# The rotary part of the latent queries: one matrix product, read crosswise, in place of two

## The chip, the cores and the metric

The kernel runs on 1 core of one Trainium2 chip. The metric is the device time of one execution in microseconds; times of several runs are given as their median.

## What is computed

Two layers of a trunk on 512 tokens of 1024 features. Each layer norms and modulates its input, makes one wide projection, runs three kinds of attention over it side by side (forgetting, latent and stick-breaking, 8 heads each), merges them through sigmoid gates, and ends with a SwiGLU network. The part that matters here is the query of the latent attention:

```python
cq = rms_norm(mla_ql, g_mla_q[l])                      # 512 x 384
q = to_heads(cq @ w_mla_uq[l], MLA_HEADS)              # 8 heads of 96
q_nope = q[..., :MLA_NOPE]                             # 64 plain
q_rope = apply_rope(q[..., MLA_NOPE:], cos[:, None], sin[:, None])   # 32 rotary

def apply_rope(x, cos, sin):
    x1, x2 = jnp.split(x.astype(jnp.float32), 2, axis=-1)
    out = jnp.concatenate([x1 * cos - x2 * sin, x1 * sin + x2 * cos], axis=-1)
```

So each rotary feature needs its own value times cos and the value of its partner, 16 features away, times sin with a sign.

## The kernel before

Features lie on the partitions and the 512 tokens on the free axis. Every float32 product is made of three passes on split numbers: `mm3` (lines 199 to 201) adds hi*hi, hi*lo and lo*hi, and `gemm` does that for each chunk of 128 input features. Weights are loaded by SP's queue four tiles deep; `divide` makes their hi with a copy on ScalarE (line 171) and their lo with a subtraction on VectorE (line 173), and runs two to three weights ahead of their use.

TensorE issues in the order in which the program is written. ScalarE, VectorE, GpSimd and the queues issue in an order that a scheduler finds at build time; the work of attention is given a lead of 30 in priority (`HP`).

The attention of a layer runs in windows, two heads each. The function `slot` goes through the eleven pieces of work of a head (the scores S of its four blocks of queries, and the transposes T and value products PV of the head before), and between them it takes steps from a queue of other matrix products: a step is three matmuls of one chunk, one unit of the queue has several. `left_steps` says how many steps the queue of a window has, and the slots spread them evenly.

Window 4 computes heads 6 and 7 (the last of the forgetting attention) and has the units `uqr` (rotary queries of latent heads 0 to 3), `uq` (plain queries of the first pair) and `ukv` (keys and values of the first pair). Window 5 computes heads 8 and 9, the first latent ones. Window 6 computes heads 10 and 11 and has the second `uqr` among its units. So there are two units of this kind in a layer, four in the kernel.

In `uqr`, the weights hold the rotary columns of four heads twice, 768 columns: once as they are, and once with the two halves of each head's 32 columns exchanged. Two products come out of it, of 128 features each. `rope_queries` multiplies the first by cos and the second by the signed sin (both with the scale of the scores) on VectorE, adds them on GpSimd, copies the hi part on ScalarE and subtracts for the lo part on GpSimd. `latent_head`, after the window, sends each head's 32 rows of hi and of lo to rows 64 to 95 of the tiles from which the head's scores are made; these transfers are issued by GpSimd. The score products of a latent head (lines 717 to 719) wait for them, and for the plain rows that lines 246, 247, 243 and 244 write.

Of the kernel before, what the change touches and what calls it, by code (L numbers as in the profile page):

```python
# [13 lines left out]
ALU = mybir.AluOpType  # L14
# [6 lines left out]
L = 2  # L21
# [11 lines left out]
# columns of the constants  # L33
C_INV, C_SGN, C_N = 0, 1, 2
# columns of the small vectors of a layer
# [4 lines left out]
# the blocks of queries whose weights ScalarE normalises  # L40
SCALE_ACT = {"f": (3,), "m": (2, 3)}
# between steps of the products: scores of a head (c), and transposes and products of the head before (p)
# [8 lines left out]
# products of constants that keep TensorE's clock up at the start  # L51
WARM = (24, 12)
# steps of products before each norm of the latents
WAIT = (8, 3, 8, 4)
# the chunk after which the rope tables are made
ROPE_AT = 4
# the chunk of the first products of the FFN after which the second half's norm comes
SS_AT = 3
# how far the work of attention goes before other work in the schedule, and steps by which the weights' division waits
HP, LAG = 30, 1  # L60

# 2*pi in parts of 8 bits, so that a product with a whole number below 2**16 is exact
# [4 lines left out]
def tile_hybrid_trunk(ctx: ExitStack, tc: tile.TileContext, xT, cvec, pos, cst, cmask, vec, gfin,  # L67
# [19 lines left out]
    # TensorE issues in the order written here; the other engines as the scheduler finds best  # L87
    ctx.enter_context(tc.manual_schedule(engines={pe.engine}))

    # ScalarE's functions, in phases of one table set each  # L90
# [15 lines left out]
    def windows(l):  # L106
        """Units of matrix products to run beside the attention of a pair of heads."""
        fox = [[("proj", l, 3 * p + i) for i in range(3)] for p in range(4)]
        sb = [[("proj", l, 12 + 3 * p + i) for i in range(3)] for p in range(4)]
        mla = [[("uqr", l, p // 2)] * (p % 2 == 0) + [("uq", l, p), ("ukv", l, p)] for p in range(4)]  # L110
        mg = [("merge", l, b, m) for b in range(3) for m in range(KC)]
        w = fox + [mla[0], mla[1] + [sb[0][0]], mla[2] + [sb[0][1]], mla[3] + [sb[1][0]], [sb[0][2], sb[1][1]]]
        w.append([mg[0], sb[1][2], mg[1], mg[2]])
        for p in range(2, 4):
            w.append([u for i in range(3) for u in (mg[3 * p - 3 + i], sb[p][i])])
        return w + [mg[9:14], mg[14:16], mg[16:]]

    def loads_of(u):
        kind, l, a = u[:3]
        if kind == "first":  # L120
            return [(w_first[l, a], NFIRST)]
        if kind == "proj":
            return [(w_proj[l, a], D)]
        if kind == "uqr":
            return [(w_uqr[l, a], 768)]
        if kind == "uq":
            return [(w_uq[l, a], 384)]
        if kind == "ukv":
            return [(w_ukv[l, a], 512)]
        if kind == "merge":  # L130
            return [(w_proj[l, 24 + a * KC + u[3]], D), (w_o[l, a * KC + u[3]], 512)]
        if kind == "out":
            return [(w_out[l, a], D)]
        if kind == "gu":
            return [(w_gu[l, a], D)]
        return [(w_dn[l, a, :, k0 * P : k1 * P], (k1 - k0) * P) for k0, k1 in KS]
# [22 lines left out]
    def divide(want, after=None):  # L159
        """hi and lo of the weights before the want-th; after: what goes before them on ScalarE and VectorE"""  # L160
# [17 lines left out]
    def W(unit, n=1, raw=3, ready=2, lag=0):  # L178
        """The next n weights, of that unit on, as (hi, lo); later ones are on their way."""
        i = at[0]  # L180
        if fourth[0]:
            raw, ready = 4, 3
        assert LOADS[i][0] == unit, (LOADS[i][0], unit)
        at[0] = i + n
        divide(i + n)

        def ahead():
            divide(i + max(n, ready + 1))
            fetch(i + max(n, raw + 1))

        if lag:
            later(lag, ahead)
        else:
            ahead()
        return splits[i] if n == 1 else splits[i : i + n]

# [6 lines left out]
    def gemm(o, wt, acts, m=P, start=True, stop=True, c0=0, cols=FULL):  # L203
        """o += W^T a over the chunks of acts, in steps; wt = (hi, lo) holds them m columns each from c0 on."""
# [19 lines left out]
    def steps(n):  # L224
        """n steps of the products in the queue"""
# [24 lines left out]
    H = S // 2  # L250

    class Norm:
        """1/sqrt(mean of squares over the features) of half the tokens, in every partition."""
# [77 lines left out]
    make_identity(nc, identf)  # L331
    # additive masks of the diagonal block: a query sees keys <= it, and keys < it
# [9 lines left out]
    # rope tables, rows alike in each 32: cos, and -sin | +sin  # L342
# [9 lines left out]
    # sin: +-r; cos: sin(pi/2 - |r|)  # L352
# [10 lines left out]
    def ada(l, i, c, wt=None, on_pool=False, after=None):  # L363
        """Column c of part i of the modulation."""
# [12 lines left out]
        if i in (1, 4):  # L377
            # g * (1 + scale)
# [16 lines left out]
    # ================= layers =================  # L395
    def values(ap, psv, name, got):
        """[2 heads' features, tokens] in PSUM -> [keys, block, head, hi | lo of the features]."""
# [14 lines left out]
    class Head:  # L412
# [4 lines left out]
        def S(self, i):  # L417
# [8 lines left out]
            if self.kind == "s":  # L426
                # sigmoid(z) of the key times the product of sigmoid(-z) over the later keys
# [20 lines left out]
        def T(self, js):  # L448
            """The weights of key blocks js, keys on the partitions, as hi and lo."""
# [12 lines left out]
        def PV(self, j):  # L462
            """[64 features, queries] += values^T weights^T; rows 0-63: hi of the values, rows 64-127: lo."""
# [12 lines left out]
    def slot(cur, prev, n):  # L476
        """The scores of a head and the rest of the head before it, between n steps of the queue."""
# [13 lines left out]
    for l in range(L):  # L491
# [32 lines left out]
        if l == 0:  # L524
# [4 lines left out]
            def warm(n):  # L529
                """Products of constants while there is nothing else: TensorE's clock falls when it idles."""  # L530
# [5 lines left out]
            # room that has no other use yet  # L536
# [65 lines left out]
        # of a head: qa = its queries' hi and lo, ka = its keys' hi twice; kb = its keys' lo  # L602
# [19 lines left out]
        def unit(u):  # L622
# [5 lines left out]
            elif kind == "uqr":  # L628
                wt = W(u, lag=LAG)
                ts = [pst("mm", f"tr{i}") for i in range(2)]  # L630
                yield from gemm(ts[0], wt, cq)
                yield
                yield from gemm(ts[1], wt, cq, c0=384)
                rope_queries(a, ts)
# [48 lines left out]
        def latent_keys(pr):  # L683
            """The rows that are alike in all heads"""
# [11 lines left out]
        def rope_queries(quad, ts):  # L696
# [4 lines left out]
            dve.scalar_tensor_tensor(qr, ts[0], sc, cosT, ALU.mult, ALU.mult)  # L701
            dve.scalar_tensor_tensor(qsf, ts[1], sc, sinT, ALU.mult, ALU.mult)
# [5 lines left out]
        def latent_head(pr):  # L708
            for hh in range(2):
                st_ = sets[pr % 2][hh * 4 : hh * 4 + 4]  # L710
                g = (pr % 2 * 2 + hh) * 32
                for a in range(2):
                    pool.dma_start(out=st_[a][64:96], in_=quads[pr // 2][a][g : g + 32])
# [28 lines left out]
        def merge(u, b, m):  # L742
            """merged[m] += sigmoid(gate) * (y_b w_o)"""
# [28 lines left out]
        def left_steps(w):  # L772
            n = {"proj": 8, "uqr": 6, "uq": 3, "ukv": 4, "merge": 12}
            return sum(n[u[0]] for u in win[w])

        # the first pair's projections, with the forget gates and the norms of the latents
        enqueue(0)
        steps(1)
        with scoped(f"fg{l}", "right") as lp:
            # log of the forget gates: min(z, 0) - ln(1 + exp(-|z|)); its sums, negated  # L780
# [183 lines left out]
def _inputs(x, c, positions, g_mix, w_ada, b_ada, w_in, b_fox_f, g_mla_q, w_mla_uq, g_mla_kv,  # L964
            w_mla_ukv, w_o_fox, w_o_mla, w_o_sb, w_out, g_ffn, w_ffn_gate, w_ffn_up, w_ffn_down, g_final):
    """The arrays of the launch: the inputs, laid out for it."""
# [5 lines left out]
    def tiles(w):  # L972
        # [L, K, N] -> [L, N / 128, 128 rows of a chunk, chunks, 128]
# [6 lines left out]
    def col(v):  # L980
        # [L, n * 128] -> [128, L, n]
# [6 lines left out]
    def qkv(w):  # L988
        # q, k, v tiles of a pair of heads, pair after pair
# [8 lines left out]
    uqr = np.stack([uq[..., 64:], np.concatenate([uq[..., 80:], uq[..., 64:80]], axis=-1)], axis=-2)  # L998
    # l kc p quad head part 32 -> l quad p part kc head 32
    uqr = uqr.reshape(L, 3, P, 2, 4, 2, 32).transpose(0, 3, 2, 5, 1, 4, 6).reshape(L, 2, P, 768)  # L1000
    ukv = np.asarray(w_mla_ukv).reshape(L, 2, P, 4, 2, 2, 64)  # l kc p pair head k|v 64
    ukv = ukv.transpose(0, 3, 2, 5, 1, 4, 6).reshape(L, 4, P, 512)

    wo = np.stack([np.asarray(w_o_fox), np.asarray(w_o_mla), np.asarray(w_o_sb)], axis=1)  # L 3 512 1024
# [15 lines left out]
    # row i: queries of the first half of block i; keys of its second half  # L1020
# [25 lines left out]
# 10000 ** (-i / 16) in float32  # L1046
# [25 lines left out]
```

## Time and profile before

| | |
|---|---|
| runs shown | 1897.41, 1897.56, 1901.94 us |
| median | 1897.56 us |
| span of the profiled execution, first to last instruction | 1895.3 us (that execution's own device time is not listed; the span is 2.3 us under the median) |
| TensorE busy | 1857.2 us, 98% |
| VectorE busy | 1169.2 us, 62% |
| ScalarE busy | 852.1 us, 45% |
| GpSimd busy | 141.8 us, 7% |

Busy time is the time covered by an engine's instructions. Matmuls are pipelined: one's record is longer than the distance to the next one's start. In the rows, L199 is line 199 of the kernel; a row of the timeline gives the start in us from the span's start, the duration in us, the engine, the line, the operation, the tile written and the tiles read, and shapes; idle time before it and what ended that stand in brackets.

### The profile page before, as it was taken

To read this page: it belongs to the slowest core of one execution; us is meant where nothing else is said; L and a number is where in the kernel's file an instruction comes from. 1 tells how busy PE (TensorE), PEld (TensorE's weight loads), DVE (VectorE), ACT (ScalarE), POOL (GpSimd) and SP (SyncE) were. 2 spreads that over 40 slices of the span, in tenths; PEclk is the share of its full clock that TensorE was granted. 3 is DMA by queue.
4 is the path that set the end of the run, shared out by engine and by line. 5 is a ranking of instruction groups with operands and counts; after the bars stand their busy time and mean duration, and the time that the engine had idled before them with its cause. 6 is when DMAs were issued, how large, how long until landed. Compare 5 with 4: busy or idle time off the path is not lost.

```text
span 1895.3 us, 24083 instructions
## 1 busy us (share of the span) xinstructions
PE 1857.2 (98%) x8956; PEld 1515.1 (80%) x8956; DVE 1169.2 (62%) x2043; ACT 852.1 (45%) x1543; POOL 141.8 (7%) x260
## 2 busy tenths in 40 slices
PE   6999999999999999999999999999999999999998
PEld 4788787777889888778897887777788888888887
DVE  8888887677756655554558898666664463333333
ACT  4767874443334322232237688544433342232321
POOL 4122100001000000000002121000110000000000
PEclk8999999999999999999999999999999999999999
DMA  7423323333642655555633222122142222223231
GB/s 276 141 73 81 82 79 117 102 110 131 208 150 70 211 177 184 171 184 194 197 107 101 66 68 85 66 84 83 68 145 99 97 100 100 95 95 98 92 92 53
DMA packets 76741, 224.22 MB, mean 118 GB/s; under 512 B 10768, under 2 KB 13968, under 8 KB 76624
## 3 DMA queue, kind: packets, MB, share of 16 engines
q1 hardware_dynamic: 69136, 213.30, 33.8%
q0 software_dynamic: 7488, 9.38, 2.5%
q8 instruction: 71, 1.16, 0.3%
q14 instruction: 46, 0.38, 0.1%
HBM read 209.20 MB, written 4.19 MB: 113 GB/s over the span
## 4 chain that ended last, share of the span: by engine, by line
PE 79%; DMA 9%; DVE 7%; issue 3%; ACT 2%; SPq 0%; DVEq 0%; POOL 0%; POOLq 0%
DMA wraw<-in_w_ada_dram 8%; PE gate L199 5%; PE gate L201 5%; PE gate L200 5%; PE proj L199 4%; PE proj L200 4%; PE dn L200 4%; PE dn L199 4%; PE dn L201 4%; PE proj L201 4%; PE o L199 3%; PE o L200 2%; PE o L201 2%; PE fu L200 2%; PE fu L199 2%
## 5 line engine op out<-in xcount | busy, mean ns | idle before, releaser
L171 ACT CAST wh<-wraw 128x1024 fp32r<-128x1024 f32 (+4 forms) x332 | 311.4, 939 | 560.3 <-PE fu L200 125.1
L173 DVE TENSOR_TENSOR wl<-wraw,wh 128x1024 fp32r<-128x1024 f32 (+4 forms) x332 | 375.8, 1132 | 230.0 <-ACT wh L171 224.7
L372 DVE CUSTOM_DVE_ANT_0 wraw<-wraw,condb 128x1024 f32<-128x1024 f32 x80 | 98.6, 1232 | 153.0 <-DMA wraw<-in_w_ada_dram 152.9
L199 PE MATMUL proj<-uh,wh 128*128 128x512 f32 x384 | 162.2, 422 | 0.0
L199 PE MATMUL gate<-uh,wh 128*128 128x512 f32 x384 | 157.8, 411 | 0.0
L201 PE MATMUL proj<-uh,wl 128*128 128x512 f32 x384 | 151.3, 394 | 0.0
L200 PE MATMUL proj<-ul,wh 128*128 128x512 f32 x384 | 151.3, 394 | 0.0
L201 PE MATMUL gate<-uh,wl 128*128 128x512 f32 x384 | 150.6, 392 | 0.0
L200 PE MATMUL gate<-ul,wh 128*128 128x512 f32 x384 | 150.6, 392 | 0.0
L199 PE MATMUL dn<-hh,wh 128*128 128x512 f32 (+1 forms) x396 | 145.5, 367 | 0.0
L200 PE MATMUL dn<-hl,wh 128*128 128x512 f32 (+1 forms) x396 | 145.4, 367 | 0.0
L201 PE MATMUL dn<-hh,wl 128*128 128x512 f32 (+1 forms) x396 | 144.4, 365 | 0.1
L201 PE MATMUL fu<-uh,wl 128*128 128x512 f32 x336 | 131.5, 391 | 1.6 <-DVE wl L173 1.6
L200 PE MATMUL fu<-ul,wh 128*128 128x512 f32 x336 | 131.0, 390 | 0.0
L199 PE MATMUL fu<-uh,wh 128*128 128x512 f32 x336 | 130.9, 389 | 0.0
L199 PE MATMUL fg<-uh,wh 128*128 128x512 f32 x320 | 125.5, 392 | 0.0
L200 PE MATMUL fg<-ul,wh 128*128 128x512 f32 x320 | 125.5, 392 | 0.0
L201 PE MATMUL fg<-uh,wl 128*128 128x512 f32 x320 | 125.5, 392 | 0.0
L199 PEld LDWEIGHTS gate<-uh,wh 128*128 128x128 f32 x384 | 72.0, 188 | 19.8 <-issue 4.8
L201 PEld LDWEIGHTS proj<-uh,wl 128*128 128x128 f32 x384 | 72.3, 188 | 16.9
L201 PEld LDWEIGHTS gate<-uh,wl 128*128 128x128 f32 x384 | 72.0, 188 | 16.7
L201 PEld LDWEIGHTS dn<-hh,wl 128*128 128x128 f32 x396 | 74.4, 188 | 13.3 <-DVE wl L173 0.5
(370 smaller groups left out, 3973.2 us busy)
## 6 DMA issues: line engine op xcount, KB each, us to landing
wraw<-in_w_proj_dram SPq DMA_DIRECT2D x96, 512.0 KB, 3.5
wraw<-in_w_gu_dram SPq DMA_DIRECT2D x88, 512.0 KB, 3.6
wraw<-in_w_ada_dram SPq DMA_DIRECT2D x80, 512.0 KB, 3.3
wraw<-in_w_dn_dram SPq DMA_DIRECT2D x32, 512.0 KB, 4.0
wraw<-in_w_o_dram SPq DMA_DIRECT2D x48, 256.0 KB, 2.6
wada<-in_w_ada_dram SPq DMA_DIRECT2D x16, 512.0 KB, 5.6
wraw<-in_w_out_dram SPq DMA_DIRECT2D x16, 512.0 KB, 3.5
wraw<-in_w_dn_dram SPq DMA_DIRECT2D x16, 384.0 KB, 3.1
```

Of the source, the lines that this page charges most:

```text
L171: ins = [act.copy(wh[:, :c], raws[j][:, :c]).ins]
L173: ins.append(dve.tensor_sub(wl[:, :c], raws[j][:, :c], wh[:, :c].bitcast(F32)).ins)
L199: pe.matmul(o, wh, ah, start=start, stop=False)
L200: pe.matmul(o, wh, al, start=False, stop=False)
L201: pe.matmul(o, wl, ah, start=False, stop=stop)
L372: ins = dve.tensor_tensor_reduce(out=wt, in0=wt, in1=condb, op0=ALU.mult, op1=ALU.add, scale=1.0, scalar=0.0, accum_out=m).ins
```

## The change

The weights of `uqr` hold each rotary column once, 384 columns, ordered so that the first halves of four heads fill features 0 to 63 and the second halves 64 to 127. One product comes out. VectorE multiplies it by cos as before; for the part with sin, two operations read the product crosswise: what goes to rows 0 to 63 is read from rows 64 to 127 and the other way round, with a constant per row (sign and scale) in a third column of the constants. Since a head's 32 rows now lie in two groups of 16, `latent_head` sends two transfers of 16 rows for each of hi and lo. The count of steps of the unit falls from 6 to 3 in `left_steps`, so the slots of windows 4 and 6 spread 10 and 18 steps in place of 13 and 21. The order of the columns of w_mla_uq and the new constants are prepared in `_inputs`.

```diff
-C_INV, C_SGN, C_N = 0, 1, 2
+C_INV, C_SGN, C_ROT, C_N = 0, 1, 2, 3
...
         if kind == "uqr":
-            return [(w_uqr[l, a], 768)]
+            return [(w_uqr[l, a], 384)]
...
             elif kind == "uqr":
-                wt = W(u, lag=LAG)
-                ts = [pst("mm", f"tr{i}") for i in range(2)]
-                yield from gemm(ts[0], wt, cq)
-                yield
-                yield from gemm(ts[1], wt, cq, c0=384)
-                rope_queries(a, ts)
+                t = pst("mm", "tr")
+                yield from gemm(t, W(u, lag=LAG), cq)
+                rope_queries(a, t)
...
-        def rope_queries(quad, ts):
+        def rope_queries(quad, t):
...
-            dve.scalar_tensor_tensor(qr, ts[0], sc, cosT, ALU.mult, ALU.mult)
-            dve.scalar_tensor_tensor(qsf, ts[1], sc, sinT, ALU.mult, ALU.mult)
+            dve.scalar_tensor_tensor(qr, t, sc, cosT, ALU.mult, ALU.mult)
+            for to, of in ((slice(0, 64), slice(64, 128)), (slice(64, 128), slice(0, 64))):
+                dve.scalar_tensor_tensor(qsf[to], t[of], csts[of, C_ROT : C_ROT + 1], sinT[of], ALU.mult, ALU.mult)
...
-                g = (pr % 2 * 2 + hh) * 32
+                g = (pr % 2 * 2 + hh) * 16
                 for a in range(2):
-                    pool.dma_start(out=st_[a][64:96], in_=quads[pr // 2][a][g : g + 32])
+                    for to, of in ((64, g), (80, 64 + g)):
+                        pool.dma_start(out=st_[a][to : to + 16], in_=quads[pr // 2][a][of : of + 16])
...
-            n = {"proj": 8, "uqr": 6, "uq": 3, "ukv": 4, "merge": 12}
+            n = {"proj": 8, "uqr": 3, "uq": 3, "ukv": 4, "merge": 12}
...
-    uqr = np.stack([uq[..., 64:], np.concatenate([uq[..., 80:], uq[..., 64:80]], axis=-1)], axis=-2)
...
-    uqr = uqr.reshape(L, 3, P, 2, 4, 2, 32).transpose(0, 3, 2, 5, 1, 4, 6).reshape(L, 2, P, 768)
+    uqr = uq[..., 64:].reshape(L, 3, P, 2, 4, 2, 16).transpose(0, 3, 2, 1, 5, 4, 6).reshape(L, 2, P, 384)
...
+        cst[r, C_ROT] = cst[r, C_SGN] * (1.0 if r < 64 else -1.0) * 96**-0.5
```

## Rows read from the trace of the kernel before

**Rows 1.** The page: span, and busy time of each engine

```profile
span 1895.3 us, 24083 instructions
...
PE 1857.2 (98%) x8956; PEld 1515.1 (80%) x8956; DVE 1169.2 (62%) x2043; ACT 852.1 (45%) x1543; POOL 141.8 (7%) x260
```

**Rows 2.** The page: the chain that ended last, shares of the span

```profile
PE 79%; DMA 9%; DVE 7%; issue 3%; ACT 2%; SPq 0%; DVEq 0%; POOL 0%; POOLq 0%
```

**Rows 3.** Busy time by stretch: windows 4, 5 and 6 of the first layer

```profile
core 0: us, PE busy (x) PEld busy (x) DVE busy (x) ACT busy (x) POOL busy (x), PEclk, DMA share, GB/s
162.61:180.45 17.84, 17.26 (x97) 14.09 (x95) 16.75 (x46) 13.90 (x35) 9.44 (x16) 1.00 0.29 78
180.45:200.94 20.49, 20.13 (x115) 16.71 (x113) 17.92 (x41) 18.03 (x43) 0.12 (x1) 1.00 0.22 63
200.94:225.66 24.72, 24.31 (x129) 19.51 (x127) 20.92 (x41) 18.48 (x43) 6.79 (x11) 1.00 0.38 107
```

**Rows 4.** Tile tr: forms, durations in ns (min/median/max), first and last start

```profile
L199 PE MATMUL tr<-cqh,wh x24: 388/424/482, 163.4 to 1133.6; 128*128 128x512 f32 x24
...
L701 DVE SCALAR_TENSOR_TENSOR qr<-tr,cosT x4: 681/686/692, 169.7 to 1132.2; 128x512 f32<-128x512 f32 x4
L702 DVE SCALAR_TENSOR_TENSOR qs<-tr,sinT x4: 682/687/692, 171.5 to 1134.5; 128x512 f32<-128x512 f32 x4
```

**Rows 5.** Timeline of TensorE: three of the product's matmuls and its last

```profile
166.75 0.40 PE L199 MATMUL tr<-cqh,wh 128*128 128x512 f32 x1
...
167.22 0.39 PE L201 MATMUL tr<-cqh,wl 128*128 128x512 f32 x1
...
171.03 0.39 PE L201 MATMUL tr<-cqh,wl 128*128 128x512 f32 x1
```

**Rows 6.** Timeline of VectorE: a crosswise 64-row operation, a 128-row one, their successors

```profile
149.20 0.68 DVE L607 SCALAR_TENSOR_TENSOR t<-proj,t 64x512 fp32r<-64x512 f32 x1
149.92 0.16 DVE L441 RECIPROCAL rif<-rsf 128x1 f32<-128x1 f32 x1
...
169.67 0.68 DVE L701 SCALAR_TENSOR_TENSOR qr<-tr,cosT 128x512 f32<-128x512 f32 x1
170.27 0.28 DVE L437 TENSOR_REDUCE nmf<-sf 128x1 f32<-128x128 f32 x1
```

**Rows 7.** Splits on VectorE (line 173): two durations, and those of head 7

```profile
189.38 0.94 DVE L173 TENSOR_TENSOR wl<-wraw,wh 128x768 fp32r<-128x768 f32 x1
...
196.49 0.55 DVE L173 TENSOR_TENSOR wl<-wraw,wh 128x384 fp32r<-128x384 f32 x1
...
171.26:180.45 9.19, 1.23 (x2) 1.00 0.43 105
```

**Rows 8.** Timeline around the end of window 4: what meets there

```profile
178.54 0.33 PE L468 MATMUL yf<-plf,vf 128*64 128x256 f32 x1 [0.39 <-DVE plf L244]
...
179.81 0.66 DVE L244 TENSOR_TENSOR t<-tk,t 64x512 fp32r<-64x512 f32 x1
...
180.68 0.40 PE L718 MATMUL sm<-t,t 96*128 96x512 f32 x1
```

**Rows 9.** Timeline of GpSimd in window 4: first addition, second transfer

```profile
172.31 1.29 POOL L703 TENSOR_TENSOR qr<-qr,qs 128x512 f32<-128x512 f32 x1 [0.94 <-DVE qs L702]
...
176.07 0.50 POOL L713 DMA_DIRECT2D t<-qs  x1
```

**Rows 10.** DMA issues from 160 to 190 us: median us to landing

```profile
t<-rh POOLq DMA_DIRECT2D x4, 64.0 KB, 2.6
t<-qs POOLq DMA_DIRECT2D x4, 64.0 KB, 2.9
```

**Rows 11.** Timeline, window 6: an addition and a split beside it; a split alone

```profile
209.24 1.28 POOL L703 TENSOR_TENSOR qr<-qr,qs 128x512 f32<-128x512 f32 x1 [28.67 <-DVE qs L702]
209.31 2.29 DVE L173 TENSOR_TENSOR wl<-wraw,wh 128x1024 fp32r<-128x1024 f32 x1
...
230.34 1.23 DVE L173 TENSOR_TENSOR wl<-wraw,wh 128x1024 fp32r<-128x1024 f32 x1
```

## The prediction

> **What bounds the kernel now.** I read the page first: of a span of 1895.3 us TensorE is busy 1857.2, VectorE 62% and ScalarE 45% [rows 1]. The chain that ended last runs for 79% of the span through TensorE [rows 2]. On the whole, then, a matmul that goes away gives back its time. The change, though, sits in two short stages of each layer, so I cut the span there: the view of busy time by stretch, with the bounds at the first score product of a head. Window 4 (heads 6 and 7) lasts 17.84 us, window 5 20.49, window 6 (heads 10 and 11) 24.72 [rows 3]. The reader should compare two columns there: TensorE is busy 17.26 of 17.84 us in window 4, and VectorE 16.75, which is 94%. VectorE is nearly as full as TensorE. In window 6 it is 20.92 of 24.72, or 85%. [...] Then I followed the tile of the two products, the order of VectorE's and GpSimd's work around it, and the waits.
>
> The times sum against the profiled span of 1895.3 us; 2.3 us lie between that and the median of 1897.56, and I take them as unchanged.
>
> **What goes from TensorE.** The first of the product's three passes has 24 matmuls [rows 4], the two others as many: 72 in four units (two a layer), 18 a unit. Half go: 9 a unit, 36 in all. One lasts about 0.39 us, but they overlap; what one costs the queue is the distance of starts, 0.47 us over two, 0.234 each [rows 5]. So 9 x 0.234 = 2.10 us a unit and 36 x 0.234 = 8.4 us in all, 0.44%. That is the most the shorter queue itself can give; the waits inside the stages come on top (0.58, 0.36 and 0.41 us of idle TensorE in windows 4, 5 and 6, as stretch less busy time [rows 3]).
>
> **What VectorE gets.** Now two operations of 128x512 a unit, 0.69 us each [rows 4]. After: one of 128x512 and two of 64x512. The trace has the very form: a 64x512 operation that reads PSUM and writes the other half of the partitions takes 0.68 us, as long as one of 128 rows, so the split of the rows saves nothing. Moreover its successor starts 0.72 us after it, while the 128-row operation lets its successor start after 0.60 [rows 6]. So 0.60 becomes 2 x 0.72 = 1.44: +0.84 us a unit. Bounds: +0.69 (one duration more) and +0.95 (0.84, and one more overlap lost behind the second).
>
> [...]
>
> **What gets lighter.** A unit's weights shrink from 768 to 384 columns: VectorE's part of the split from 0.94 to 0.55 us [rows 7], -0.39, ScalarE's a little, the load by half. But these splits lie one window earlier (the 768-column one of window 6 is done at 189.38, in window 5), so they don't relieve the window that gets the 0.84. Count them as 0 to 0.36 us in window 5, whose idle TensorE they could fill; I take 0.
>
> **DMAs.** Each head's rows come in four transfers in place of two for hi and lo: 32 more in all. An issue of 32 rows holds GpSimd 0.50 us [rows 9]; for 16 rows I take as much (half of it if it went by rows): 8 us a layer more on an engine that is busy 7% of the span. Bytes are the same. Hidden by GpSimd's idle time, unless a head waits for them (below).
>
> **Window 4, once shortened.** TensorE's queue needs 17.84 - 2.10 = 15.74 us. VectorE's busy time becomes 16.75 + 0.84 = 17.59, so VectorE is now the longer. What can slide out of the window are two splits of weights for window 5, 1.23 us [rows 7]: 16.36. Without any gap VectorE would thus let the window end 17.84 - 16.36 = 1.48 us sooner: the best case. If nothing slides and VectorE keeps the 17.84 - 16.75 = 1.09 us that it now waits, the window grows by 0.84: the worst. Two rows say which is nearer. TensorE already waits here for VectorE (0.39 us before a product of values), and the first head of window 5 starts its second score product at 180.68, when VectorE has finished that head's low part of the keys at 180.47 [rows 8]: TensorE would have to be 2 us earlier there, and VectorE can't. With the gaps kept and the splits gone: 17.84 - (16.36 + 1.09) = 0.39. I take 0.2 us gained (bounds -0.84 and +1.48).
>
> **Window 6.** TensorE's queue becomes 24.72 - 2.10 = 22.62, VectorE 20.92 + 0.84 = 21.76, 96% of it. Here TensorE stays the longer, but as full a VectorE as that cost window 4 0.58 us of waits, so I take 2.10 - 0.5 = 1.6 gained. Bounds: +2.5 (2.10 and the 0.41 of idle time too) and +0.8 (1.3 us of waits, three times today's).
>
> **Window 5** gets the splits that slid: VectorE has 20.49 - 17.92 = 2.57 us free there, so nothing to -0.6 (half of 1.23); I take 0.
>
> Sum: 0.2 + 0 + 1.6 = 1.8 us a layer, 3.6 in two. Bounds: (1.48 + 0.36 + 2.5) x 2 = 8.7 us gained, and (-0.84 - 0.6 + 0.8) x 2 = 1.3 us lost. So 1897.56 - 3.6 = **1894.0 us**, between 1888.9 and 1898.8.
>
> **Rivals.** *TensorE's queue decides everywhere.* VectorE's order is found anew for the changed kernel, and there may be more to slide than I see: then about 7.4 us, nearly all of the 8.4, are gained: 1890.2. For it: the 98% of [rows 1]. Against: window 4's 94% of VectorE.
>
> *The additions on GpSimd meet VectorE's work on SBUF.* A split of 128x1024 takes 2.29 us beside GpSimd's addition of the rope parts, and 1.23 alone [rows 11]; that is window 6 now, where TensorE absorbs most of it. In window 4 the two additions now fall (172.31 for the first [rows 9]) on VectorE operations that read PSUM. The product is finished three steps earlier after the change, and the additions move to other neighbours. If both hit operations on SBUF alone in window 4, the bound engine gets up to 2 x 1.06 = 2.1 us more; 1.9 taken, in both layers, eats the 3.6: 1897.8, no change.
>
> [...]
>
> *Slower: head 8 waits for its rope rows.* Today its second transfer is issued at 176.07 [rows 9] and lands 2.9 us later [rows 10], at 179.0; the head starts at 180.45, a slack of 1.5. After: the product ends 3 steps sooner (its ninth matmul starts at 167.22 [rows 5], the last of the second product at 171.03), VectorE takes 0.84 more, and the last of now four transfers is issued 1.0 later: 179.0 - 3.8 + 0.84 + 1.0 = 177.0, for a head that starts 0.2 to 2.1 us sooner. So it decides only if VectorE leaves the rope work, which yields to the attention's, more than 1.3 to 3.2 us longer than it could. Should it leave it 6 us, head 8 waits 2.8 to 4.7, and two layers lose 5.6 to 9.4 us against the 3.6: 1899.6 to 1903.4, 1901 taken. Against it: today the first product waits only 2.0 us for VectorE (last matmul 167.22 and 0.39; started at 169.67 [rows 6]).
>
> **How the numbers follow.** Under 0.3% (5.7 us) a time can't be told from no change. My forecast 0.55, TensorE everywhere 0.25, the meeting on SBUF 0.11, head 8 0.09. Faster by over 0.3% (below 1891.9): the second case, 0.25, and 0.03 of the forecast's tail. Slower (above 1903.3): 0.04, the worse half of the last. Same: 0.68. The range takes the bounds of the sum, 1888.9 and 1898.8, which hold the first three cases; widened to 1888.5 and 1899.5 it leaves out the last case and little else.
>
> **What the profile after would show.** 36 matmuls of this product in place of 72; three operations of VectorE a unit, the crosswise ones 0.68 long and 0.72 apart; window 4 within 0.5 us of 17.84 with VectorE over 96% busy; window 6 near 23.1; 64 transfers of rope rows at 0.5 us each. Window 4 near 15.8 would refute the central step, that VectorE takes over there; a wait of a head's first score product for a DMA would show the last rival; splits over 2 us in window 4 the one before it.

## The result and the profile after

The changed kernel takes 1903.47 us (median of 20 runs, 1899.22 to 1911.84); the kernel before, run beside it, 1898.91 (20 runs, 1895.70 to 1901.94). The ratio is 1.0027, 95% interval 1.0018 to 1.0035: slower by about a quarter of a per cent, 9.5 us above the forecast of 1894.0 and above the upper end of the range, 1899.5. Of the 9.5 us, 1.35 are the kernel before itself, which the forecast took at 1897.56.

The page of the changed kernel, span, busy times and the chain that ended last (before: [rows 1, 2]):

```profile
span 1901.4 us, 24079 instructions
...
PE 1851.9 (97%) x8920; PEld 1510.7 (79%) x8920; DVE 1172.3 (62%) x2047; ACT 852.1 (45%) x1543; POOL 158.0 (8%) x292
...
PE 86%; DVE 6%; DMA 4%; issue 2%; ACT 2%; POOL 0%; SPq 0%; DVEq 0%; POOLq 0%
```

The 36 matmuls are gone (8956 to 8920), yet TensorE's busy time fell by 5.3 us where they were priced at 8.4 (nearly all of the rest is window 5 of both layers, 1.4 us each at a lower granted clock, below), and the span grew by 6.1. The whole page can't say more; the stages can. Windows 4, 5 and 6 of the first layer in the changed kernel, columns as in [rows 3], and in the last line head 8 alone:

```profile
core 0: us, PE busy (x) PEld busy (x) DVE busy (x) ACT busy (x) POOL busy (x), PEclk, DMA share, GB/s
162.73:183.07 20.34, 15.70 (x87) 12.15 (x86) 18.76 (x47) 14.82 (x36) 9.19 (x15) 1.00 0.21 52
183.07:204.62 21.55, 21.55 (x114) 18.01 (x115) 17.15 (x40) 17.33 (x41) 4.39 (x10) 0.92 0.26 67
204.62:229.66 25.04, 21.91 (x119) 17.89 (x118) 21.93 (x42) 18.42 (x43) 10.66 (x18) 1.00 0.38 105
183.07:194.32 11.25, 11.25 (x56) 9.35 (x56) 9.69 (x22) 9.87 (x22) 4.39 (x10) 0.85 0.36 85
```

Beside [rows 3]: window 4 is 2.50 us longer (17.84 to 20.34), window 5 1.06 (20.49 to 21.55), window 6 0.32 (24.72 to 25.04). TensorE's busy time fell by 1.56 us in window 4 and by 2.40 in window 6 (2.10 each were forecast), but where it had 0.58 us without work in window 4 it now has 4.64, and in window 6 3.13 in place of 0.41. In window 5 it has no gap at all: there its 114 matmuls themselves take longer (21.55 us, where 115 took 20.13), at a granted clock of 0.92. The second layer repeats the three lengths to 0.05 us, and that of the kernel before repeats its own to 0.02 (17.85, 20.48 and 24.70, at a granted clock of 1.00 in each). With 0.3 us in window 3, whose cause is open, a layer loses 4.2 us, two 8.4. The profiled span lost 6.1; the other 2.3 came back between the two layers, in a stretch of some 798 us that the change does not touch and that lies between 795.9 and 800.5 us in the profiles of the kernels that keep these units in place. The medians differ by 4.6 only. The runs without a profile show no stages, but each has its mean granted clock, and the time mostly goes with it: of the changed kernel's 20 runs the fastest, 1899.22 us, has 0.995, and the six at 0.992 or less take 1905.1 to 1911.8 (two at 0.994 take 1905.9 and 1906.8 as well). So part of the loss comes and goes with the clock.

Where the gaps lie. Timeline of TensorE in the changed kernel, the matmuls ahead of which it waited; in brackets the idle time and what ended it:

```profile
166.19 0.45 PE L471 MATMUL yf<-plf,vf 128*64 128x512 f32 x1 [0.79 <-DVE plf L244]
...
173.45 0.63 PE L457 MATMUL ptf<-identf,pf 128*128 128x128 f32 x4 [1.53 <-DVE pf L445]
...
180.55 0.34 PE L468 MATMUL yf<-plf,vf 128*64 128x256 f32 x1 [1.01 <-DVE plf L244]
...
183.07 0.76 PE L717 MATMUL sm<-t,t 100*128 100x512 f32 x1 [1.14 <-DMA t<-rh]
...
217.55 0.63 PE L457 MATMUL ptm<-identf,pm 128*128 128x128 f32 x4 [1.56 <-DVE pm L445]
...
220.78 0.47 PE L199 MATMUL proj<-uh,wh 128*128 128x512 f32 x1 [1.57 <-DVE t L247]
```

The first four and one of 0.18 make window 4's 4.65 us, the last two window 6's 3.13. Four of the six shown are for attention's operands that VectorE makes, one (220.78) for VectorE's reading of another product, and one (183.07) for the transfer of a head's rope rows: head 8, first score product.

What VectorE did. Its timeline in the changed kernel, windows 4 and 6:

```profile
171.32 0.76 DVE L701 SCALAR_TENSOR_TENSOR qs<-tr,csts,sinT 64x512 f32<-64x512 f32 x1
172.11 0.16 DVE L441 RECIPROCAL rif<-rsf 128x1 f32<-128x1 f32 x1
172.30 0.68 DVE L474 TENSOR_TENSOR y<-yf,y 64x512 f32<-64x512 f32 x1
173.02 0.29 DVE L445 TENSOR_SCALAR pf<-pf,rif 128x128 f32<-128x128 f32 x1
173.22 0.29 DVE L423 TENSOR_TENSOR sf<-sf,mcaus 128x128 f32<-128x128 f32 x1
173.54 0.74 DVE L701 SCALAR_TENSOR_TENSOR qs<-tr,csts,sinT 64x512 f32<-64x512 f32 x1
174.32 0.69 DVE L437 TENSOR_REDUCE nmf<-sf 128x1 f32<-128x512 f32 x1
...
177.11 0.55 DVE L173 TENSOR_TENSOR wl<-wraw,wh 128x384 fp32r<-128x384 f32 x1
...
177.84 1.52 DVE L173 TENSOR_TENSOR wl<-wraw,wh 128x512 fp32r<-128x512 f32 x1
...
213.97 2.24 DVE L173 TENSOR_TENSOR wl<-wraw,wh 128x1024 fp32r<-128x1024 f32 x1
216.13 1.28 DVE L445 TENSOR_SCALAR pm<-pm,rim 128x128 f32<-128x128 f32 x1
```

And GpSimd's, window 4 (line 702 is the addition, 704 the subtraction, 713 the transfers):

```profile
174.44 1.28 POOL L702 TENSOR_TENSOR qr<-qr,qs 128x512 f32<-128x512 f32 x1 [2.67 <-DVE qs L701]
177.20 1.62 POOL L704 TENSOR_TENSOR qs<-qr,rh 128x512 fp32r<-128x512 f32 x1 [1.48 <-ACT rh L703]
178.76 1.03 POOL L713 DMA_DIRECT2D t<-rh  x2
179.79 0.96 POOL L713 DMA_DIRECT2D t<-qs  x2
```

Four things are to be seen. The two splits of weights for window 5, which the forecast let slide out of window 4, are both still in it (177.11 and 177.84; head 8 starts at 183.07). The two crosswise operations do not stand together: between them come 1.43 us of attention's work (172.11 to 173.54), so the addition, which needs both, starts at 174.44 and not, as before, at 172.31 [rows 9]. The transposes at 173.45 waited 1.53 us for the scaling at 173.02, ahead of which VectorE had a crosswise operation and an output to add. And beside GpSimd's subtraction (177.20 to 178.82) a split of 128x512 takes 1.52 us, where one alone takes 0.67 (177.77 in the kernel without GpSimd's operations, below).

### The profile page after: what moved, and what is told of

Same layout as the page of the kernel before. It is cut to its first block, busy times and chain, and to the rows that moved or that the text cites. A ratio compares the mean times of both kernels' runs of the same rounds, so it can differ in the third digit from the quotient of the medians.

```text
span 1901.4 us, 24079 instructions
## 1 busy us (share of the span) xinstructions
PE 1851.9 (97%) x8920; PEld 1510.7 (79%) x8920; DVE 1172.3 (62%) x2047; ACT 852.1 (45%) x1543; POOL 158.0 (8%) x292
## 4 chain that ended last, share of the span: by engine, by line
PE 86%; DVE 6%; DMA 4%; issue 2%; ACT 2%; POOL 0%; SPq 0%; DVEq 0%; POOLq 0%
PE gate L199 5%; PE gate L200 5%; PE gate L201 5%; PE proj L199 4%; PE proj L200 4%; PE dn L200 4%; PE dn L199 4%; PE dn L201 4%; PE proj L201 4%; PE fu L200 3%; PE fu L201 3%; PE fu L199 3%; PE fg L200 3%; PE fg L199 3%; PE fg L201 3%; PE o L199 3%
```

## The experiments

All times are medians beside runs of the kernel before on the same chip (1898.35, 1898.96 or 1898.45 us, by chip), with the ratio to it and its 95% interval. The ratio is not the quotient of the two medians; the two differ by up to 0.0008, which lies within the intervals. Stage lengths are windows 4, 5, 6 of layer 1 unless said otherwise.

**The halved product alone.** The sin part is made in one operation of 128 rows, so that the exchange of the halves is left out, and each head's rows go in one transfer for hi and one for lo:

```diff
-            for to, of in ((slice(0, 64), slice(64, 128)), (slice(64, 128), slice(0, 64))):
-                dve.scalar_tensor_tensor(qsf[to], t[of], csts[of, C_ROT : C_ROT + 1], sinT[of], ALU.mult, ALU.mult)
+            dve.scalar_tensor_tensor(qsf, t, sc, sinT, ALU.mult, ALU.mult)
...
-                    for to, of in ((64, g), (80, 64 + g)):
-                        pool.dma_start(out=st_[a][to : to + 16], in_=quads[pr // 2][a][of : of + 16])
+                    pool.dma_start(out=st_[a][64:96], in_=quads[pr // 2][a][2 * g : 2 * g + 32])
```

> The changed kernel with the sin part as one 128-row operation (no exchange of halves) and two transfers of 32 rows a head, so only the product is halved; the rotary queries it makes are not those of the reference. Before, windows 4, 5 and 6 took 17.84, 20.49 and 24.72 us; after the change 20.34, 21.55 and 25.04. If VectorE's extra operation is the cause: window 4 at 16.5 to 17.8, the kernel 2 to 6 us faster than before. If the shorter queue alone uncovers VectorE's chains: window 4 stays at 19 or more, the kernel 2 us or more slower. If the transfers are the cause: window 4 near 17.8 with no wait for a DMA.

Measured: 1896.10 us, 0.9996 (0.9984 to 1.0007). Busy time by stretch of this kernel: windows 4, 5, 6 of layer 1, and window 5 of layer 2:

```profile
164.74:182.30 17.56, 15.17 (x88) 12.38 (x86) 16.04 (x43) 13.80 (x33) 8.83 (x15) 1.00 0.25 55
182.30:205.62 23.32, 21.71 (x115) 18.01 (x115) 18.45 (x43) 18.35 (x44) 0.87 (x2) 0.93 0.23 65
205.62:228.94 23.32, 21.91 (x119) 17.81 (x118) 20.15 (x41) 18.36 (x43) 6.76 (x11) 1.00 0.42 113
...
1108.14:1129.89 21.75, 20.12 (x115) 16.66 (x114) 18.29 (x43) 18.23 (x44) 0.87 (x2) 1.00 0.25 71
```

Window 4 gains 0.28 us and window 6 1.40. The forecast has 0.2 and 1.6 there, but for a kernel that also carries VectorE's extra operation: that the numbers are alike is luck. Window 5, taken at 0, loses 1.26 in layer 2 and 2.83 in layer 1. Its waits on TensorE's timeline, the last of window 4 and the first of window 5:

```profile
175.54 0.63 PE L457 MATMUL ptf<-identf,pf 128*128 128x128 f32 x4 [1.60 <-DVE pf L445]
...
184.30 0.50 PE L716 MATMUL sm<-t,t 96*128 96x512 f32 x1 [1.61 <-DVE t L244]
```

TensorE gets to head 8 sooner and waits there 1.61 us for the low part of the keys, VectorE's work: the second score product of head 8, which [rows 8] had shown as the point that VectorE can't bring forward. VectorE's timeline there:

```profile
182.31 0.68 DVE L173 TENSOR_TENSOR wl<-wraw,wh 128x512 fp32r<-128x512 f32 x1
...
183.58 0.66 DVE L244 TENSOR_TENSOR t<-tk,t 64x512 fp32r<-64x512 f32 x1
```

The keys are done 19.50 us after the window's start, in place of 17.86 in the kernel before (180.47 [rows 8] and 162.61 [rows 3]): they even fall behind. Of the two splits for window 5 one, of 512 columns, has moved to the window's end (182.31), and it stands there ahead of the keys. Layer 2 has the same two waits (1.61 and 1.62). The 1.57 us between the two windows 5 is the granted clock alone: 0.93 and 21.71 us of busy time for 115 matmuls, 1.00 and 20.12 for as many. So the halved product by itself returns nothing that can be told from noise: VectorE's stretch from window 4 into head 8 sets its end.

**One edit put back at a time.** From the changed kernel: the sin part in one operation but four transfers a head (the first half of the diff above), and the crosswise operations but two transfers (its second half).

> The changed kernel with the sin part as one 128-row operation (no exchange of halves), but four transfers a head. If VectorE's extra operation is the cause: as q_only within 0.5 us in each window. If the transfers are: window 4 near 19 with a wait of about 1 us of head 8's first score product for a DMA, and the clock falls behind it. If the shorter queue is: window 4 at 19 or more, whatever the transfers.

> The changed kernel with two transfers of 32 rows a head (the wrong rows of the exchanged layout), the crosswise operations kept. If VectorE's extra operation is the cause: window 4 stays at 19.5 to 20.5. If the transfers are: window 4 falls to 18.5 or less and the wait for a DMA goes. If the shorter queue is: 19 or more.

Measured: with four transfers and no crosswise operation 1900.03 us, 1.0006 (0.9997 to 1.0016); windows 17.55, 23.31, 23.34, the same as with two. In layer 2 window 4 took 19.83, with a wait of 1.83 us, ahead of the product of values at 1105.25, for an operation of ScalarE that the other kernels don't have; why is open. In the changed kernel GpSimd's addition of that window starts at 1102.76, behind two transfers ahead of which GpSimd stood 2.84 us with no wait that the profile shows. With the crosswise operations and two transfers: 1902.18 us, 1.0025 (1.0015 to 1.0034), nearly all of the changed kernel's loss. Windows 4, 5 and 6 of that kernel, and the first wait of TensorE in its window 5:

```profile
161.07:180.12 19.05, 15.54 (x87) 12.31 (x86) 17.47 (x44) 13.60 (x32) 7.88 (x12) 1.00 0.21 48
180.12:201.46 21.34, 20.27 (x115) 16.41 (x114) 18.19 (x43) 18.30 (x45) 2.09 (x5) 1.00 0.28 74
201.46:226.51 25.05, 21.97 (x119) 17.92 (x118) 21.93 (x42) 18.43 (x43) 6.99 (x11) 1.00 0.36 105
...
181.59 0.50 PE L717 MATMUL sm<-t,t 96*128 96x512 f32 x1 [1.07 <-DVE t L244]
```

Against the halved product alone, the crosswise operations make window 4 1.49 us longer and window 6 1.73, 3.2 together where 0.84 a unit, 1.7, was charged. VectorE's busy time grew by 1.43 and 1.78. By the number only the third expected case is met (19 or more, the shorter queue), and the halved product alone, at 17.56, speaks against that one; the wait for a DMA is gone. The four transfers, on top of the crosswise operations, add 1.29 to window 4 (19.05 to 20.34), 0.21 to window 5 and nothing to window 6; without the crosswise operations they add nothing to any of the three in layer 1. In the changed kernel they start late, at 178.76, and head 8 waits 1.14 us for them. But that wait is not what they cost: with two transfers head 8 waits 1.07 us one product later, for the keys, and TensorE's waits in windows 4 and 5 together are 4.6 us in both kernels. What differs is the granted clock of window 5, 0.92 against 1.00, and with it TensorE's busy time, 21.55 against 20.27 us. Both layers show it, in one profile of each kernel; why the clock falls in one and not in the other is open, and between the ratios, 1.0027 and 1.0025, it can't be seen.

**The same two edits on the kernel before**, whose product stays double (it needs no exchange, so the queries differ from the reference's; the work is the same in amount as in the changed kernel): the crosswise pair with four transfers, and the pair alone.

```diff
-            dve.scalar_tensor_tensor(qsf, ts[1], sc, sinT, ALU.mult, ALU.mult)
+            for to, of in ((slice(0, 64), slice(64, 128)), (slice(64, 128), slice(0, 64))):
+                dve.scalar_tensor_tensor(qsf[to], ts[1][of], csts[of, C_SGN : C_SGN + 1], sinT[of], ALU.mult, ALU.mult)
...
-                    pool.dma_start(out=st_[a][64:96], in_=quads[pr // 2][a][g : g + 32])
+                    for to, of in ((64, g // 2), (80, 64 + g // 2)):
+                        pool.dma_start(out=st_[a][to : to + 16], in_=quads[pr // 2][a][of : of + 16])
```

> The kernel before, two products and its queue of steps kept, with the sin part as two crosswise 64-row operations on the second product and four transfers of 16 rows a head; its rotary queries are wrong ones. If VectorE's extra operation or the transfers are the cause by themselves: window 4 at 19 or more (17.84 before), the kernel 3 us or more slower than before. If the shorter queue has to come with them: window 4 at 17.8 to 18.3, the kernel within 2 us of before.

> The kernel before with the sin part as two crosswise 64-row operations on the second product, transfers as before (two of 32 rows); its rotary queries are wrong ones. With the transfers too, windows 4, 5 and 6 took 22.3, 21.5 and 25.9 us. If the extra operation carries that cost: window 4 at 20.5 or more and window 6 at 25.5 or more. If it is the transfers: window 4 at 18.5 or less.

Measured: 1911.52 us, 1.0071 (1.0054 to 1.0087), with both; 1909.50, 1.0060 (1.0042 to 1.0079), with the crosswise pair alone. The pair alone makes windows 4, 5 and 6 of layer 2 3.2, 1.0 and 1.2 us longer (21.02, 21.47, 25.89): 5.4 a layer, three times the 2 x 0.84 charged. (In layer 1, at granted clocks of 0.89 and 0.88, windows 4 and 5 took 22.59 and 22.57.) This kernel shows the price most plainly, in one wait of window 4. VectorE's timeline there, in layer 1:

```profile
174.75 0.74 DVE L703 SCALAR_TENSOR_TENSOR qs<-tr,csts,sinT 64x512 f32<-64x512 f32 x1
...
175.87 1.48 DVE L173 TENSOR_TENSOR wl<-wraw,wh 128x384 fp32r<-128x384 f32 x1
...
177.93 1.57 DVE L445 TENSOR_SCALAR pf<-pf,rif 128x384 f32<-128x384 f32 x1
179.42 0.54 DVE L244 TENSOR_TENSOR plf<-ptf,phf 128x384 fp32r<-128x384 f32 x1
```

GpSimd's and TensorE's, the same stretch:

```profile
175.65 1.28 POOL L704 TENSOR_TENSOR qr<-qr,qs 128x512 f32<-128x512 f32 x1 [5.97 <-DVE qs L703]
...
177.99 1.28 POOL L706 TENSOR_TENSOR qs<-qr,rh 128x512 fp32r<-128x512 f32 x1
...
180.02 0.47 PE L468 MATMUL yf<-plf,vf 128*64 128x256 f32 x1 [3.38 <-DVE plf L244]
```

The second crosswise operation is done at 175.49, the addition starts at 175.65 and a split of 384 columns beside it takes 1.48 us, alone 0.55 [rows 7]; the subtraction starts at 177.99, and a scaling of 384 columns beside it takes 1.57, where one alone takes 0.41 (178.35 in the kernel without GpSimd's operations, below). That is 0.93 + 1.16 = 2.1 us, on the way to the low part of the weights at 179.42, for which TensorE had been waiting 3.38 us.

**Without GpSimd's two operations.** From the changed kernel:

```diff
-            pool.tensor_add(qr, qr, qsf)
...
-            pool.tensor_sub(qs, qr, rh.bitcast(F32))
```

> The changed kernel without GpSimd's two operations on the rope parts: the sum of the cos and the sin part and the low part are left out (hi is a copy of the cos part, the sin part is sent in place of lo). If GpSimd's operations and VectorE's on SBUF hold each other up, and so make the extra operation dear: no split or scaling of VectorE lasts over 1.3 us, window 4 falls from 20.3 to 18.5 or less and window 6 from 25.0 to 23.5 or less. If it is only VectorE's order (short operations queued behind the crosswise ones): windows 4 and 6 stay within 0.5 us of the changed kernel, save for the wait of head 8 for its transfer, 1.1 us.

> The same kernel as no_pool, for a profile at the clock of the others: the sum of the rope parts and the low part are left out on GpSimd. If GpSimd's operations and VectorE's hold each other up: no split or scaling of VectorE in windows 4 and 6 lasts over 1.3 us, window 4 at 18.5 or less, window 6 at 23.5 or less. If it is VectorE's order alone: windows 4 and 6 within 0.5 us of the changed kernel's 20.3 and 25.0, save for head 8's wait of 1.1 us.

Measured: 1896.94 us, 0.9994 (0.9984 to 1.0004), and again 1896.73, 0.9990 (0.9980 to 1.0000). The rows are from the second, whose mean granted clock, 0.993, is that of the other kernels. Windows 4 and 6:

```profile
162.94:181.81 18.87, 15.34 (x87) 12.36 (x86) 17.12 (x44) 14.35 (x33) 7.88 (x17) 1.00 0.27 63
203.04:225.92 22.88, 21.75 (x120) 18.00 (x118) 19.79 (x42) 18.22 (x43) 7.86 (x17) 1.00 0.41 115
```

Two splits on VectorE, which in the changed kernel took 1.52 and 2.24 us, and a scaling of 384 columns:

```profile
177.77 0.67 DVE L173 TENSOR_TENSOR wl<-wraw,wh 128x512 fp32r<-128x512 f32 x1
178.35 0.41 DVE L445 TENSOR_SCALAR pf<-pf,rif 128x384 f32<-128x384 f32 x1
...
212.01 1.21 DVE L173 TENSOR_TENSOR wl<-wraw,wh 128x1024 fp32r<-128x1024 f32 x1
```

Window 6 is 2.16 us shorter than in the changed kernel, window 4 1.47; the expectation of 23.5 or less is met in window 6, that of 18.5 or less is missed in window 4 (18.87). In window 6 the meetings are thus more than the whole loss, and the gain comes out near the forecast's (22.88; 23.1 was forecast). But the kernel before has these meetings too: its split of 1024 columns takes 2.29 us [rows 11], and behind it GpSimd's subtraction meets two scalings. Those two in the kernel before, and without GpSimd's operations:

```profile
211.71 1.39 DVE L445 TENSOR_SCALAR pm<-pm,rim 128x256 f32<-128x256 f32 x2
...
213.13 0.55 DVE L445 TENSOR_SCALAR pm<-pm,rim 128x256 f32<-128x256 f32 x2
```

The two meetings cost VectorE 1.9 us there (2.29 for 1.21, 1.39 for 0.55) and 2.0 in the changed kernel (2.24 for 1.21, 1.28 for 0.29). So the change did not bring them into window 6: it cut the queue of TensorE that had hidden them and added to VectorE's work beside them (TensorE: 0.41 us without work before, 3.13 after). In window 4 two things went together, the meeting with the split and head 8's wait for its transfers, which now leave earlier; beside the kernel with two transfers, which has the meeting and no such wait, only 0.18 us are gained (19.05 to 18.87). And the wait ahead of the transposes stays, 1.59 us for 1.53; so it does with one operation of 128 rows (1.60 above). That one is VectorE's order against a TensorE that comes sooner, neither the meeting nor the crossing.

**The first unit earlier.** The `uqr` of window 4 goes to window 3; then, in the next kernel, the projections of the last part, which lie in windows 5 to 8, move one window forward as well, so that window 4 keeps as many steps:

```diff
-        mla = [[("uqr", l, p // 2)] * (p % 2 == 0) + [("uq", l, p), ("ukv", l, p)] for p in range(4)]
+        mla = [[("uqr", l, p // 2)] * (p == 2) + [("uq", l, p), ("ukv", l, p)] for p in range(4)]
+        fox[3] = [("uqr", l, 0)] + fox[3]
...
-        w = fox + [mla[0], mla[1] + [sb[0][0]], mla[2] + [sb[0][1]], mla[3] + [sb[1][0]], [sb[0][2], sb[1][1]]]
+        w = fox + [mla[0] + [sb[0][0]], mla[1] + [sb[0][1]], mla[2] + [sb[1][0]], mla[3] + [sb[1][1]], [sb[0][2]]]
```

> The changed kernel with the first unit of rotary queries moved to the front of window 3 (27 steps there, 7 in window 4); it computes the reference. If what hurts is the rope work inside the fullest window: window 3 takes 24.4 + 2.1 = 26.5 us, window 4 falls to 17 or less, head 8 waits for no transfer, and the three windows 4 to 6 lose 3 us a layer against the changed kernel, of which 2.1 go to window 3. If the missing steps of TensorE are what uncovers VectorE there: window 4 stays at 18 or more with only 7 steps.

> As early, and each unit of the stick-breaking projections moved one window ahead, so that windows 4 to 8 have 15, 15, 18, 15 and 8 steps; it computes the reference. If VectorE's chains in windows 4 to 6 lacked steps to hide behind: no wait over 1 us in windows 4 to 6, and the kernel is 4 to 8 us faster than before. If the lack only moves on: window 8 with 8 steps takes on waits of 2 to 4 us a layer, and the kernel is within 3 us of before.

> The kernel before (two products) with the same two moves: the first rotary unit in window 3 (30 steps there), the stick-breaking projections one window ahead. It computes the reference. If the halved product is worth its 8.4 us once there is room: spread is 6 to 8 us faster than this one. If the crosswise operations and transfers take the gain in any order: spread is within 3 us of this one.

Measured: the unit earlier 1901.76 us, 1.0016 (1.0006 to 1.0026); with the projections 1894.17, 0.9978 (0.9969 to 0.9986); the same order on the kernel before 1900.38, 1.0008 (1.0000 to 1.0017), which is 6.2 us above the changed one in that order. Moving alone frees little: window 4, seven steps long now, still takes 17.40 us, between the two expectations (17 and 18), with a wait of 1.99 for the scaling, behind which matmuls of 512 columns start up to 0.43 us apart (0.23 ahead of it). With steps to fill it, 19.77 us hold fifteen steps. Window 6, which keeps its unit, stays at 24.80 with the same two waits (1.28 and 1.57); none over 1 us was expected there.

**Both units earlier.** The units go to windows 2 and 3, where TensorE has no gaps, the projections as above; `rope_queries` then writes to tiles that are free at that time:

```diff
+        mla = [[("uq", l, p), ("ukv", l, p)] for p in range(4)]
+        for p in range(2):
+            fox[2 + p] = [("uqr", l, p)] + fox[2 + p]
...
-            qr = rp.tile([P, S], F32, tag="qr", name="qr")
+            qr = y[1][2]
```

> The changed kernel with both rotary units moved out of the latent windows (to the fronts of windows 2 and 3, 27 steps each) and the stick-breaking projections one window ahead, as in spread; windows 4 to 8 have 15, 15, 15, 15 and 8 steps. Two of its tiles lie in room that the latent outputs use later. It computes the reference. If rope work inside VectorE's full windows was the cost: window 6 loses its two waits of 1.3 and 1.6 us and falls from 24.8 to 20.5 or less, for 2.1 more in window 2: 2 us a layer less than spread, 4 in all, some 8 us faster than before. If the missing steps are: window 6, now with 15 steps, keeps waits of 2 us or more, and the time stays within 2 us of spread.

> The kernel before with the same moves as spread2: two products a unit, at the fronts of windows 2 and 3 (30 steps each). It computes the reference. If the halved product gives its 8.4 us where TensorE alone is the limit: spread2 is 7 to 9 us faster than this one. If the crosswise operations and the transfers take part of it even there: 0 to 5.

Measured: the halved product in this order 1888.46 us, 0.9951 (0.9937 to 0.9965), the double one 1896.35, 0.9992 (0.9984 to 1.0001). Windows 3, 4 and 6 of the first:

```profile
140.56:167.07 26.51, 26.51 (x138) 21.86 (x137) 23.59 (x52) 17.19 (x39) 9.40 (x16) 1.00 0.30 86
167.07:186.84 19.77, 19.10 (x107) 15.62 (x105) 18.43 (x48) 15.89 (x39) 6.14 (x13) 1.00 0.31 78
...
206.43:226.00 19.57, 19.57 (x111) 16.36 (x109) 16.92 (x38) 16.97 (x41) 5.06 (x11) 1.00 0.37 95
```

Window 3 carries a rope unit with both crosswise operations and both GpSimd operations and has no gap: TensorE is busy 26.51 of 26.51 us, VectorE 89%. Between the two kernels of this order lie 1896.35 - 1888.46 = 7.9 us, nearly the 8.4 that 36 matmuls cost. The change is worth nearly its full price where TensorE has the longer queue; this version beats both kernels.

## Why the prediction was wrong

**What held.** 36 matmuls fewer at 0.234 us: the last pair shows 7.9 of 8.4. VectorE takes over in window 4: of TensorE's 4.65 us of waits there 3.5 are for VectorE, though it is busy 92% of the longer window and not over 96%. The 16-row transfer's issue costs what a 32-row one does: two in 0.96 to 1.03 us in window 4, where one of 32 rows took 0.50 [rows 9].

**The step that failed** is the sums by window, first of all the term "What can slide out of the window are two splits of weights for window 5, 1.23 us". In the changed kernel nothing slid: both splits stand in window 4 (177.11 and 177.84), and the second, beside GpSimd's subtraction, takes 0.85 us more than alone. That is 2.1 us on VectorE which the sum did not have; it gave 17.45 (17.84 - 0.39, of which 0.2 was taken), and the window took 20.34, or 19.05 with two transfers. Without GpSimd's operations both splits stand there as well (177.77 is the second), and it takes 18.87: 1.42 over the sum, of which 1.23 are the term. Window 6 was to gain 1.6 with 0.5 us of waits taken from window 4's row and 1.3 at the worst; TensorE waits 3.13 there, and the window lost 0.32. Window 5, taken at 0, lost 1.06.

The price of VectorE's extra operation, "+0.84 us a unit", was sized nearly right: the operation lasts 0.74 and 0.76 us in place of 0.68 (the row it was read from, line 607 [rows 6], has one constant for all rows, not one per row), and its successors start 0.79 and 0.78 us behind it, so 0.60 became 1.57: +0.97, just past the upper bound of 0.95. That bound counts the overlap behind the second operation as lost too, and the rows show no overlap behind either: each successor starts 0.03 or 0.04 us after the operation's end. But 0.97 a unit is 1.9 us a layer, and the crosswise edit alone cost 2.8 (3.2 in windows 4 and 6, less 0.4 in window 5) beside the short queue and 5.4 beside the long one. What else the sums had wrong:

- *GpSimd's two operations meet VectorE's SBUF work.* This was the rival with 0.11, priced at 1.9 us a layer and put into window 4. The sign that I named for it, a split of over 2 us in window 4, did not come: the split there takes 1.52 for 0.67. Window 6 has one of 2.24, as it had before (2.29). Taken out, window 6 gives back 2.16, which I had thought TensorE would absorb, as it did before, and window 4 at most 1.47, beside the kernel with two transfers 0.18. Beside those operations the splits, which have two SBUF inputs, take longer, and so does the scaling of line 445, which has one tensor: 1.57 for 0.41 and 1.28 for 0.29. A reduction of 128x512 that reads PSUM takes 0.69 beside the addition (174.32 in the changed kernel), as without (0.68 in the kernel before). By what the two engines hold each other up no run shows. I had counted splits only.
- *Head 8 waits for its rope rows.* The rival with 0.09; it happened, at 1.14 us in layer 1 and 1.06 in layer 2, in place of the 2.8 to 4.7 I gave it. As a wait it costs next to nothing, since head 8 would else wait 1.07 for its keys. I had the last transfer land 2.0 us earlier than before, with VectorE's delay as one number of 0.84. In fact the crosswise operations came 2.22 us apart, since the attention's work goes ahead, the subtraction ran to 178.82, and the first transfer left at 178.76, later than the second one before (176.07).
- *Window 5 was taken at 0 and lost 1.06.* Two causes, one after the other. With the halved product alone, head 8's second score product waits 1.61 us for VectorE's keys; the sentence on [rows 8] had said that VectorE can't bring these forward, but the sum used it for window 4 only, not for the time that is then lost behind its end. In the changed kernel head 8 waits for its transfers first and that wait is gone; what shows instead is the granted clock: TensorE, idle for 4.64 us of window 4, gets a granted clock of 0.85 in head 8 and of 0.92 over window 5, and is busy 21.55 us for 114 matmuls in place of 20.13 for 115 [rows 3]. No term of the sum had this. It does not follow the waits strictly: with two transfers there are 4.6 us of waits in windows 4 and 5 too, and the clock is 1.00 in both layers; the two layers of the halved product alone have the same waits and clocks of 0.93 and 1.00.

Added up for a layer, by the kernels that differ in one edit (layer 2, windows 4 to 6): halved product -0.3, +1.3, -1.3; crosswise operations +1.5, -0.4, +1.7; four transfers +1.3, +0.2, 0.0. These are differences along one chain of kernels, so they add up to the changed kernel's 3.9 (here 4.0, rounded) whatever the causes; in another order each edit would have another price, as the 5.4 beside the long queue shows. Of the 1.5 of the four transfers 1.27 are TensorE's longer busy time in window 5 (21.57 for 20.30), at a granted clock of 0.92 for 1.00. Why the clock falls stays open, and the medians show little more than half of the profiles' 8.4 us.

## What to carry to other kernels

Before matmuls are taken out of a stage, look at what else is nearly full there: in window 4, where VectorE was 94% busy, nine matmuls fewer gave 0.3 us and the next stage lost 1.3 (the halved product alone, layer 2), while the same ones taken out of stages with TensorE at 100% gave 7.9 of 8.4 us in all. Before an engine's work is counted as sliding into the next stage, check that nothing puts it first: here two splits stayed. A delay that a long queue hides can come out when the queue is cut: GpSimd's meetings with VectorE on SBUF cost VectorE 1.9 us in window 6 before and 2.0 after, and TensorE's time without work there went from 0.41 to 3.13 us. Follow what starts after an added operation (here GpSimd's work and the transfers for the next head). If the edit can go to where that engine has room, fill the place that it leaves: against the kernel before, the ratio of the changed kernel went from 1.0027 to 1.0016 with one unit moved alone, to 0.9978 with the place filled, and to 0.9951 with both units moved.

## What the runs showed of the hardware

- A VectorE operation of 64x512 that reads PSUM crosswise with a constant per row takes 0.74 to 0.76 us; with one constant for all rows a crosswise one takes 0.68 (line 607 [rows 6]), as a 128x512 one without the crossing does. Its successor doesn't overlap it (0.77 to 0.79 us between starts).
- Beside a GpSimd operation on two SBUF tensors (1.28 to 1.62 us), VectorE's scalings, not only its subtractions, took up to 1.16 us more (128x384: 1.57 for 0.41).
- After waits of some 4.6 us within one window, TensorE's granted clock was 0.85 over the next 11.25 us, though it had no gap in them; with two transfers in place of four, 3.5 us of waits in that window and 1.07 behind its end left it at 1.00. With the halved product alone both layers have the same waits, and windows 5 at 0.93 and 1.00, 1.57 us apart.
